# A hybrid decoder layer on one core: first gate and up passes taken by quarters in turn, state-space parameters loaded behind the statistics

## The chip, the core and the metric

The kernel runs on one core of a Trainium2 chip. The metric is the device time of one execution in microseconds (us), as the median of repeated runs. Engines are called as the profile calls them: PE (TensorE, matrix products; PEld is its loading of weights), DVE (VectorE), ACT (ScalarE), POOL (GpSimd) and SP (SyncE, which here only issues transfers). Each of them works through its own list of instructions in order.

## The reference, cut to what matters

One layer for 256 tokens of width 2048, all in float32:

```python
x = x + 0.5 * SwiGLU(RMSNorm(x))        # D_FF = 5632: gate, up, down
h = RMSNorm(x) @ W_in                   # q | k | v | u
x = x + concat(attention(q, k, v), GLU(S5(u))) @ W_out
x = x + 0.5 * SwiGLU(RMSNorm(x))

def swiglu_ffn(x, w_gate, w_up, w_down):
    return (silu(x @ w_gate) * (x @ w_up)) @ w_down
```

S5 is a state-space recurrence over 64 channel groups. Its discretised matrices depend on parameters alone (lambda, dt, B, C), so the kernel can work them out at any time before the mixer.

## The kernel before, in words

**Passes, groups, half groups.** Every weight matrix is read once. A pass (class `Pass`) is one block of 512 output columns. It multiplies all 256 tokens, as two tiles `t` of 128 rows, and gathers in two PSUM banks of 128x512, one for each tile (`acc`). It goes through the weight rows in groups of four 128-row tiles; a group is one transfer of 1 MB into a `raw` buffer, and there are three such buffers (`RAWB`). A pass over 2048 input features has four groups, called quarters here. Each group is worked in two half groups. For a half group ACT copies the raw weights, rounded, to `wh` (L286), DVE computes the rest `wl = raw - wh` (L291; L289 in halves for the first two groups), and PE does 12 products of 128x128 by 128x512: for two k tiles and two token tiles `xh*wh`, `xh*wl` and `xl*wh` (L330, L331, L332). The activations are split alike into `xth` and `xtl`. Four `wh`/`wl` pairs exist (`WB`), so ACT and DVE can be at most some three half groups ahead of PE.

**Who sets the order.** The order is written out by hand. `run` walks through the groups; `ahead` emits transfers and splits ahead of the products. After each half group `step` advances every spawned generator by one yield: everything else (normalisation, statistics, the turning of hidden values, state-space parameters) is such a generator, and a number that it yields is how many half groups it sits out.

**The start.** The input `x` is fetched as four column quarters (`res0` to `res3`, by `load_x` between the weight transfers on SP). `Normed.feed` transposes a quarter on PE (L189), and `close` scales it by the gain and splits it on ACT (L170) and DVE (L173). `warm_up` puts transposes of the identity on PE while nothing else is there. The row statistics (`squares`, L158 on ACT; `count`, ending in twelve small POOL instructions, L118 to L121) are needed only when the first gate pass is done: Silu (L363) takes 1/rms as its scale. Four accumulator banks exist (`accp`), two for each pass.

**Feed-forward 1.** It has 11 chunks `c` of 512 hidden columns, each a gate pass and an up pass. Behind an up pass DVE multiplies (L374), transposes 32x32 blocks (L134, `blocks`), and SP sends them through HBM and back (`h_d<-blocks`, L137; `sil<-h_d`, four transfers, L140); then ACT and DVE split the turned chunk (L124 and L125, `hid`). This is called the turn of chunk `c`. A turn's ACT instruction stands in ACT's list among the weight copies.

**State-space parameters** (`ssm_prepare`). POOL first issues the loads of all parameters (L433 to L449). Long chains of small DVE instructions follow, and then four pieces: in each, eight steps of three DVE products (L655 to L657), DVE transposes (L670), transfers of 1 MB from POOL (`m_d`: L667 and L673), products on PE, and on SP small transfers `k_d` (L688) and `t_d` (L691). For chunks 5 and up the turn waits until `ssm_prepare` has ended; the gate pass of chunk 7 forces its end.

The functions that the change touches and their callers:

Of the kernel before, what the change touches and what calls it, by code (L numbers as in the profile page):

```python
# [46 lines left out]
def hybrid_layer_kernel(  # L47
# [8 lines left out]
    act, vec, pe, pool, sync = nc.scalar, nc.vector, nc.tensor, nc.gpsimd, nc.sync  # L56
# [25 lines left out]
    def tps():  # L82
        return tpp.tile([P, 512], F32, name=nm("tp"), tag="tp")
# [3 lines left out]
    res = [const.tile([P, NT, 512], F32, name=f"res{n}", tag=f"res{n}") for n in range(4)]  # L87
# [135 lines left out]
    def spawn(g, delay=0):  # L223
        gens.append([g, delay])
        return g
# [22 lines left out]
    def finish(*gs):  # L248
        while any(alive(g) for g in gs):
            step()  # L250

    def run(passes, extra, start):
        groups = []
        for p in passes:
            for k0 in p.ks:
                groups.append((p, k0))
        ng = len(groups)
# [51 lines left out]
        for i, (p, k0) in enumerate(groups):  # L309
            if k0 == p.ks[0]:  # L310
                if p.pre:
                    p.pre()
                if p.opens:
                    p.box["acc"] = [tps() if p.bank == "tp" else
                                    accp.tile([P, 512], F32, name=nm("acc"), tag="acc") for _ in range(NT)]
                acc = p.box["acc"]
            for s in range(2):
                u = 2 * i + s
                ahead(u)
                h, l = wts.pop(u)  # L320
                order = [(kk, t) for kk in range(2) for t in range(NT)]
                if s == 1 and k0 == p.ks[-1]:
                    order = [(kk, t) for t in range(NT) for kk in range(2)]
                for kk, t in order:
                    k = k0 + 2 * s + kk
                    sh, sl = p.stat(k)
                    first = p.opens and k == p.ks[0]
                    last = p.done is not None and k == p.ks[-1] + 3
                    c = slice(t * P, (t + 1) * P)
                    pe.matmul(acc[t], sh[:, c], h[:, kk, :], start=first, stop=False)  # L330
                    pe.matmul(acc[t], sh[:, c], l[:, kk, :], start=False, stop=False)  # L331
                    pe.matmul(acc[t], sl[:, c], h[:, kk, :], start=False, stop=last)  # L332
                if s == 1 and k0 == p.ks[-1] and p.done:
                    spawn(call(p.done, acc), p.delay)
                step()
# [735 lines left out]
    with tc.manual_schedule():  # L1071
        xin = x[0].rearrange("(t p) d -> p t d", p=P)
        grow = slots.tile([50, P], F32, name="grow", tag="s5a")
        act.dma_start(out=grow[0:16], in_=ffn1_norm[0].rearrange("(k p) -> k p", p=P))
        sync.dma_start(out=res[0][:, :, 0:256], in_=xin[:, :, 0:256])
        vec.memset(warm, 0.0)
        act.activation(out=warm, in_=warm, func=AF.Silu)
        make_identity(nc, ident)

        def warm_up(n):  # L1080
            ps = tps()
            for _ in range(n):
                pe.transpose(ps[:, 0:P], ident, ident)

        warm_up(12)
        ps = tps()
        pe.transpose(ps[:, 0:16], grow[0:16], ident[:16, :16])
        vec.tensor_copy(out=gains["f1"], in_=ps[:, 0:16])

        def other_gains():  # L1090
            for i, g in enumerate((mix_norm, ffn2_norm)):
                pool.dma_start(out=grow[16 + 16 * i:32 + 16 * i], in_=g[0].rearrange("(k p) -> k p", p=P))
            pool.dma_start(out=grow[48:49], in_=q_norm)
            pool.dma_start(out=grow[49:50], in_=k_norm)
            pool.memset(flip, 0.0)
            pool.affine_select(out=flip, in_=flip, compare_op=ALU.not_equal, fill=1.0, base=1 - P,
                               pattern=[[1, P]], channel_multiplier=1)
            pool.memset(sgn[0:64], 1.0)
            pool.memset(sgn[64:128], -1.0)
            yield 4  # L1100
            ps = tps()
            pe.transpose(ps[:, 0:50], grow, ident[:50, :50])
            for i, key in enumerate(("mx", "f2")):
                vec.tensor_copy(out=gains[key], in_=ps[:, 16 + 16 * i:32 + 16 * i])
            knc = small([P, 1], "knc")
            vec.tensor_copy(out=knc, in_=ps[:, 49:50])
            vec.scalar_tensor_tensor(out=qkg, in0=ps[:, 48:49], scalar=1.0 / math.sqrt(HD), in1=knc,
                                     op0=ALU.mult, op1=ALU.mult)
            yield
            yield from bias_table()  # L1110

        def bias_table():
            rel = small([34, NH], "rel")
            pool.memset(rel, 1.0)  # L1114
            pool.dma_start(out=rel[0:32], in_=rel_bias)
            oh = slots.tile([34, SPAN], F32, name="oh", tag="s1a")
            pool.dma_start(out=oh, in_=bias_rows)
            yield
            yield
            ps = tps()  # L1120
            pe.matmul(ps[:NH, 0:SPAN], rel, oh, start=True, stop=True)
            bt = slots.tile([NH, SPAN], F32, name="bt", tag="s1b")
            vec.tensor_copy(out=bt, in_=ps[:NH, 0:SPAN])
            pool.dma_start(out=b_d, in_=bt)

        n1, nmix, n2 = Normed("f1"), Normed("mx"), Normed("f2")

        feeds = [n1.feed(n, True) for n in range(4)]

        def feed_input():  # L1130
            for n in range(1, 4):
                for _ in feeds[n]:
                    pass
                yield 2 if n < 3 else 1
            spawn(other_gains())
            mx["pre"] = spawn(ssm_prepare(), 1)
            for n in range(4):
                n1.squares(n)
                n1.count()
                yield  # L1140

        def start():
            next(feeds[0], None)
            if "go" not in mx:
                warm_up(4)
            if "go" in mx:
                spawn(feed_input())
            mx["go"] = True

        ff1 = ffn(n1, ffn1_w_gate[0], ffn1_w_up[0], ffn1_w_down[0], residual(nmix, 0.5), True)  # L1150
        mixp = mixer(nmix, residual(n2, 1.0))
        ff2 = ffn(n2, ffn2_w_gate[0], ffn2_w_up[0], ffn2_w_down[0], lambda n: final(n), False)

        def load_x(n):
            if n == 0:
                sync.dma_start(out=res[0][:, :, 256:512], in_=xin[:, :, 256:512])
            elif n < 4:
                sync.dma_start(out=res[n], in_=xin[:, :, n * 512:(n + 1) * 512])

        run(ff1 + mixp + ff2, load_x, start)  # L1160


# [52 lines left out]
```

## Time and profile before

| | us |
|---|---|
| median of three runs | 1836.66 |
| the runs | 1832.95, 1836.66, 1837.66 |
| the profiled execution | 1833.54 |
| its span, first to last instruction | 1831.8 |
| mean granted PE clock in it | 0.992 |

The span is shorter than the execution by 1.7 us, which lie around the program. Views of waits name the waiting instruction first, then what released it, then the total, the count and the longest. A timeline row has the start, the busy time, engine, line, operation and tiles, and in brackets the idle time ahead of it with what ended it. A row of the view of stretches has, behind its bounds and length, the busy time of each engine with its number of instructions, then the granted PE clock, the busy share of the transfer engines and GB/s.

### The profile page before, as it was taken

How to read it: one execution, taken by the hardware profiler on the slowest of the kernel's cores; microseconds unless marked ns; L12 is line 12 of the kernel's file. 1: busy time of each engine (PE TensorE's matmuls, PEld its weight loads, DVE VectorE, ACT ScalarE, POOL GpSimd, SP SyncE). 2: the span in 40 equal slices, each digit the busy share in tenths (PEclk: the TensorE clock that was granted, in tenths of full speed). 3: DMA queues.
4: the chain of work that ended last, by engine and by line, in shares of the span. 5: the costliest groups of instructions: out<-in, count | busy, mean ns of one | idle time of the engine just before them, and what ended most of it. 6: DMA issues, size and time to landing. Idle time of an engine off the chain costs nothing.

```text
span 1831.8 us, 21467 instructions
## 1 busy us (share of the span) xinstructions
PE 1798.0 (98%) x8389; PEld 1476.9 (81%) x8389; DVE 1060.3 (58%) x1382; ACT 834.7 (46%) x1071; POOL 43.4 (2%) x91
## 2 busy tenths in 40 slices
PE   8999999999999999989999999999999999999999
PEld 6788777788888888868878888888888888888887
DVE  4778788555554555534795665555555555544443
ACT  5444344444444444435667555444444444443332
POOL 2100000000000000010000001000000000000000
PEclk8999999999999999989999999999999999999999
DMA  8665788867776666599656586677767767665662
GB/s 270 208 213 191 254 264 283 262 211 213 224 218 215 209 219 216 186 255 302 186 156 250 197 246 212 195 232 217 224 212 217 219 210 225 208 222 202 202 211 103
DMA packets 220389, 401.23 MB, mean 219 GB/s; under 512 B 9580, under 2 KB 50133, under 8 KB 219136
## 3 DMA queue, kind: packets, MB, share of 16 engines
q1 hardware_dynamic: 214384, 383.29, 65.7%
q0 software_dynamic: 4080, 13.43, 2.4%
q10 hardware_dynamic: 1824, 3.15, 0.7%
q8 instruction: 65, 1.06, 0.2%
q14 instruction: 36, 0.29, 0.0%
HBM read 370.00 MB, written 32.45 MB: 220 GB/s over the span
## 4 chain that ended last, share of the span: by engine, by line
PE 84%; DVE 8%; DMA 5%; ACT 1%; issue 1%; SPq 1%; ACTq 0%; DVEq 0%
PE acc L330 27%; PE acc L331 27%; PE acc L332 27%; DVE wl L291 3%; DMA h_d<-blocks 2%; DMA sil<-h_d 1%; DMA raw<-in_ffn_w_gate_dram 1%; DVE s4b L655 1%; ACT wh L286 1%; DMA raw<-in_w_in_dram 1%; DVE s1a L768 1%; DVE s1a L769 0%; DVE slot L656 0%; DVE s4a L657 0%; DVE s4a L656 0%
## 5 line engine op out<-in xcount | busy, mean ns | idle before, releaser
L291 DVE TENSOR_TENSOR wl<-raw,wh 128x1024 fp32r<-128x1024 f32 x628 | 764.6, 1225 | 635.0 <-ACT wh L286 634.5
L286 ACT ACTIVATE wh<-raw 128x1024 fp32r<-128x1024 f32 (+1 forms) x636 | 666.2, 1057 | 820.6 <-PE acc L332 762.5
L330 PE MATMUL acc<-wh,xth 128*128 128x512 f32 x1664 | 658.7, 396 | 16.5 <-ACT wh L286 16.5
L331 PE MATMUL acc<-wl,xth 128*128 128x512 f32 x1664 | 653.9, 393 | 3.6 <-DVE wl L291 3.2
L332 PE MATMUL acc<-wh,xtl 128*128 128x512 f32 x1664 | 652.0, 392 | 0.0
L330 PEld LDWEIGHTS acc<-wh,xth 128*128 128x128 f32 x1664 | 314.9, 189 | 85.1 <-ACT wh L286 19.0
L331 PEld LDWEIGHTS acc<-wl,xth 128*128 128x128 f32 x1664 | 315.0, 189 | 74.0 <-DVE wl L291 9.7
L332 PEld LDWEIGHTS acc<-wh,xtl 128*128 128x128 f32 x1664 | 314.8, 189 | 66.1
L331 PE MATMUL acc<-wl,hid 128*128 128x512 f32 x704 | 274.0, 389 | 0.0
L330 PE MATMUL acc<-wh,hid 128*128 128x512 f32 x704 | 274.0, 389 | 0.0
L332 PE MATMUL acc<-wh,hid 128*128 128x512 f32 x704 | 273.9, 389 | 0.0
L331 PEld LDWEIGHTS acc<-wl,hid 128*128 128x128 f32 x704 | 132.1, 188 | 27.5
L332 PEld LDWEIGHTS acc<-wh,hid 128*128 128x128 f32 x704 | 132.1, 188 | 27.5
L330 PEld LDWEIGHTS acc<-wh,hid 128*128 128x128 f32 x704 | 132.1, 188 | 27.3
L125 DVE TENSOR_TENSOR hid<-sil,hid 128x512 fp32r<-128x512 f32 x44 | 28.5, 688 | 79.6 <-ACT hid L124 79.6
L124 ACT ACTIVATE hid<-sil 128x512 fp32r<-128x512 f32 x44 | 25.4, 624 | 99.4 <-DMA sil<-h_d 99.4
L374 DVE SCALAR_TENSOR_TENSOR sil<-acc,rstd,sil 128x512 f32<-128x512 f32 x44 | 30.8, 741 | 0.0
L363 ACT ACTIVATE sil<-acc,rstd 128x512 f32<-128x512 f32 x44 | 27.5, 674 | 3.8 <-POOL rel L1114 3.8
L134 DVE STREAM_TRANSPOSE blocks<-sil 128x512 f32<-128x512 f32 x44 | 28.5, 685 | 0.0
L118 POOL TENSOR_TENSOR rs_t<-rstd 128x2 f32<-128x2 f32 x9 | 5.7, 632 | 659.8 <-DVE rstd L115 659.3
L330 PE MATMUL acc<-wh,slot 128*128 128x512 f32 x48 | 18.9, 393 | 0.0
L331 PE MATMUL acc<-wl,slot 128*128 128x512 f32 x48 | 18.7, 389 | 0.0
(324 smaller groups left out, 791.0 us busy)
## 6 DMA issues: line engine op xcount, KB each, us to landing
raw<-in_ffn_w_up_dram SPq DMA_DIRECT2D x88, 1024.0 KB, 5.9
raw<-in_ffn_w_down_dram SPq DMA_DIRECT2D x88, 1024.0 KB, 5.1
raw<-in_ffn_w_gate_dram SPq DMA_DIRECT2D x87, 1024.0 KB, 5.9
raw<-in_w_in_dram SPq DMA_DIRECT2D x32, 1024.0 KB, 5.6
raw<-in_w_out_dram SPq DMA_DIRECT2D x16, 1024.0 KB, 5.6
h_d<-blocks SPq DMA_DIRECT2D x28, 512.0 KB, 7.0
sil<-h_d SPq DMA_DIRECT2D x88, 128.0 KB, 7.3
m_d<-slot POOLq DMA_DIRECT2D x4, 1024.0 KB, 7.0
```

Source lines behind the costliest of these rows:

```text
L124: act.activation(out=h, in_=src, func=AF.Copy)
L125: vec.tensor_tensor(out=l, in0=src, in1=h.bitcast(F32), op=ALU.subtract)
L134: vec.transpose(out=b[:, :, t].rearrange("p j (k c) -> p j k c", k=4), in_=src[:, t, :].rearrange("p (k j c) -> p j k c", k=4, j=4))
L286: act.activation(out=h[:, c], in_=src[:, c], func=AF.Copy)
L291: vec.tensor_tensor(out=l, in0=src, in1=h.bitcast(F32), op=ALU.subtract)
L330: pe.matmul(acc[t], sh[:, c], h[:, kk, :], start=first, stop=False)
L331: pe.matmul(acc[t], sh[:, c], l[:, kk, :], start=False, stop=False)
L332: pe.matmul(acc[t], sl[:, c], h[:, kk, :], start=False, stop=last)
L363: act.activation(out=sil[c][:, t, :], in_=acc[t], func=AF.Silu, scale=norm.scale(t))
L374: vec.scalar_tensor_tensor(out=a[:, t, :], in0=acc[t], scalar=norm.scale(t), in1=a[:, t, :], op0=ALU.mult, op1=ALU.mult)
L655: vec.tensor_tensor(out=t_, in0=zb, in1=pr, op=ALU.mult)
L768: vec.tensor_tensor(out=tm, in0=a8, in1=prev.unsqueeze(1).broadcast_to([P, 2, 2, NG]), op=ALU.mult)
```

## The change

The first eight groups are taken in another order: gate quarter 0, up quarter 0, gate 1, up 1, gate 2, gate 3, up 2, up 3. Both passes of chunk 0 are open at once, so all four accumulator banks are in use until Silu has read the gate's two. The input's quarters 1, 2 and 3 are fetched after weight groups 1, 3 and 4 of the new order. Their transposition comes at other half groups. The statistics of a quarter are taken between the quarters' feeds and no longer all behind them. `other_gains` and `ssm_prepare` are spawned after the statistics and no longer before them; so on POOL the twelve statistics instructions stand ahead of the parameter loads. The second warm-up has 14 transposes in place of 4.

```diff
     def run(passes, extra, start):
-        groups = []
-        for p in passes:
+        g, u = passes[:2]
+        groups = [(g, 0), (u, 0), (g, 4), (u, 4), (g, 8), (g, 12), (u, 8), (u, 12)]
+        for p in passes[2:]:
             for k0 in p.ks:
                 groups.append((p, k0))
...
-                acc = p.box["acc"]
+            acc = p.box["acc"]
...
             for n in range(1, 4):
                 for _ in feeds[n]:
                     pass
-                yield 2 if n < 3 else 1
+                yield
+                n1.squares(n - 1)
+                n1.count()
+                yield 3 if n == 1 else 1
+            n1.squares(3)
+            n1.count()
+            yield
             spawn(other_gains())
             mx["pre"] = spawn(ssm_prepare(), 1)
-            for n in range(4):
-                n1.squares(n)
-                n1.count()
-                yield
 
         def start():
             next(feeds[0], None)
             if "go" not in mx:
-                warm_up(4)
+                warm_up(14)
             if "go" in mx:
-                spawn(feed_input())
+                spawn(feed_input(), 2)
             mx["go"] = True
...
-            elif n < 4:
-                sync.dma_start(out=res[n], in_=xin[:, :, n * 512:(n + 1) * 512])
+            elif n in (2, 4, 5):
+                c = (n + 1) // 2
+                sync.dma_start(out=res[c], in_=xin[:, :, c * 512:(c + 1) * 512])
```

Three places show what this does to the lists; lines of the changed kernel are 1 higher from the head of `run` on, and 4 higher at the end. First SP at its start, where `res` are the input's quarters and `raw` the weight groups. Before:

```order
L1075 DMA res_83<-in_x_dram 128x2x256
L269 DMA raw_144<-in_ffn_w_gate_dram 128x512 x2
L1156 DMA res_83<-in_x_dram 128x2x256
L271 DMA raw_144<-in_ffn_w_gate_dram 128x2x512
L1158 DMA res_84<-in_x_dram 128x2x512
L273 DMA raw_150<-in_ffn_w_gate_dram 128x4x512
L1158 DMA res_85<-in_x_dram 128x2x512
L273 DMA raw_153<-in_ffn_w_gate_dram 128x4x512
L1158 DMA res_86<-in_x_dram 128x2x512
L273 DMA raw_193<-in_ffn_w_gate_dram 128x4x512
```

Now:

```order
L1076 DMA res_83<-in_x_dram 128x2x256
L270 DMA raw_144<-in_ffn_w_gate_dram 128x512 x2
L1159 DMA res_83<-in_x_dram 128x2x256
L272 DMA raw_144<-in_ffn_w_gate_dram 128x2x512
L274 DMA raw_149<-in_ffn_w_up_dram 128x4x512
L1162 DMA res_84<-in_x_dram 128x2x512
L274 DMA raw_152<-in_ffn_w_gate_dram 128x4x512
L274 DMA raw_201<-in_ffn_w_up_dram 128x4x512
L1162 DMA res_85<-in_x_dram 128x2x512
L274 DMA raw_228<-in_ffn_w_gate_dram 128x4x512
L1162 DMA res_86<-in_x_dram 128x2x512
```

A group of the up pass, which works on the input quarter that is already there, now comes between the gate's quarters, and each further input quarter is asked for later.

Second, SP at the turn of chunk 2 (`h_d`, `sil`) and the first state-space piece (`k_d`, `t_d`). Before:

```order
L137 DMA h_d_107<-blocks_1478 128x4x256
L273 DMA raw_1526<-in_ffn_w_up_dram 128x4x512
L140 DMA sil_494<-h_d_107 32x4x256 x4
L273 DMA raw_1569<-in_ffn_w_gate_dram 128x4x512
L688 DMA k_d<-slot_63_420 16x4x128 x4
L273 DMA raw_1635<-in_ffn_w_gate_dram 128x4x512
L691 DMA t_d<-k_d 256x1x128 x8
```

Now:

```order
L137 DMA h_d_107<-blocks_1470 128x4x256
L274 DMA raw_1518<-in_ffn_w_up_dram 128x4x512
L140 DMA sil_555<-h_d_107 32x4x256 x4
L274 DMA raw_1564<-in_ffn_w_gate_dram 128x4x512
L274 DMA raw_1610<-in_ffn_w_gate_dram 128x4x512
L274 DMA raw_1650<-in_ffn_w_gate_dram 128x4x512
L274 DMA raw_1687<-in_ffn_w_gate_dram 128x4x512
L689 DMA k_d<-slot_86_560 16x4x128 x4
L274 DMA raw_1749<-in_ffn_w_up_dram 128x4x512
L692 DMA t_d<-k_d 256x1x128 x8
```

The turn stands where it stood; the piece comes three weight groups, that is six half groups, later.

Third, DVE at the same turn: L134 are its block transposes, L655 to L657 the piece's products, `wl` the weight splits. Before:

```order
L291 TENSOR_TENSOR wl_1460<-raw_1358,wh_1459 128x1024
L655 TENSOR_TENSOR s4b_422<-s2a_418,slot_63_420 128x256
L656 TENSOR_TENSOR s4a_421<-s2a_418,slot_63_420 128x16x16
L657 TENSOR_TENSOR s4a_421<-s4a_421,s4b_422 128x16x16
L134 STREAM_TRANSPOSE blocks_1478<-sil_494 128x4x128 x2
L291 TENSOR_TENSOR wl_1482<-raw_1358,wh_1481 128x1024
```

Now:

```order
L637 TENSOR_TENSOR dmask<-dmask,ident 128x16
L638 TENSOR_TENSOR dmask<-dmask,ident 128x16
L292 TENSOR_TENSOR wl_1450<-raw_1344,wh_1449 128x1024
L656 TENSOR_TENSOR s4b_562<-s2a_558,slot_86_560 128x512
L657 TENSOR_TENSOR s4a_561<-s2a_558,slot_86_560 128x16x32
L658 TENSOR_TENSOR s4a_561<-s4a_561,s4b_562 128x16x32
L134 STREAM_TRANSPOSE blocks_1470<-sil_555 128x4x128 x2
L292 TENSOR_TENSOR wl_1474<-raw_1344,wh_1473 128x1024
```

The transposes stood behind the seventh of the piece's eight steps; they stand behind the first. From the turn of chunk 6 on the lists of both kernels agree.

## The prediction

> **What bounds the kernel now.** I read the head of the page first, then the timeline at the places where the view of waits has PE waiting.
>
> ```profile
> span 1831.8 us, 21467 instructions
> PE 1798.0 (98%) x8389; PEld 1476.9 (81%) x8389; DVE 1060.3 (58%) x1382; ACT 834.7 (46%) x1071; POOL 43.4 (2%) x91
> ```
>
> PE sets the time: it is busy for 98% and idle for 34 us. The change neither adds nor removes a product, so it can only remove or add waits and slow clock. Behind the turn of chunk 6 both lists agree; only what lies ahead of it, some 370 us, can change. The start in the timeline:
>
> ```profile
> 5.24 0.92 PE L1083 MATMUL tp<-ident 128*128 128x128 f32 x4
> 8.35 0.63 PE L189 MATMUL tp<-ident,res 128*128 128x128 f32 x4 [2.18 <-DMA res<-in_x_dram]
> 20.82 2.19 ACT L286 ACTIVATE wh<-raw 128x512 fp32r<-128x512 f32 x4 [5.46 <-DMA raw<-in_ffn_w_gate_dram]
> 21.50 0.79 PE L330 MATMUL acc<-wh,xth 128*128 128x512 f32 x1 [4.54 <-ACT wh L286]
> 30.38 0.39 PE L330 MATMUL acc<-wh,xth 128*128 128x512 f32 x1
> 33.10 1.03 PE L189 MATMUL tp<-ident,res 128*128 128x128 f32 x8
> ...
> 5.00:10.00 5.00, 2.82 (x15) 2.40 (x14) 2.19 (x5) 2.86 (x7) 3.96 (x7) 0.93 0.86 283
> 10.00:15.00 5.00, 5.00 (x22) 4.01 (x22) 2.30 (x5) 2.11 (x6) 3.04 (x5) 0.73 1.06 251
> 20.00:25.00 5.00, 3.50 (x8) 2.48 (x9) 2.50 (x4) 2.19 (x4) 0.00 (x0) 0.50 1.04 385
> 25.00:30.00 5.00, 5.00 (x25) 4.16 (x24) 2.94 (x4) 3.46 (x6) 0.00 (x0) 0.86 1.05 387
> ```
>
> A half group takes 33.10 - 30.38 = 2.72 us at full clock, a feed's eight transposes 1.0. PE stands 4.54 us for the gate's second quarter of weights. Behind each pause the granted clock falls: 0.93 and 0.73 after the pause at 6.2 to 8.3, 0.50 and 0.86 after the second. The first costs 0.07 x 5 + 0.27 x 5 = 1.7 us. The second costs 0.5 x 3.5 (PE works from 21.5) + 0.14 x 5 = 2.4.
>
> Why are the weights late?
>
> ```profile
> DMA packets 1681, 2.35 MB, mean 235 GB/s; under 512 B 236, under 2 KB 811, under 8 KB 1681
> ...
> q0 software_dynamic: 784, 1.82, 23.1%
> raw<-in_ffn_w_gate_dram SPq DMA_DIRECT2D x3, 1024.0 KB, 18.0
> ```
>
> By 10 us 2.35 MB had come; in the first 30 us POOL's queue q0 moved 1.82 MB, mostly of parameters, while a weight group took 18.0 us to land. From 20 us on, without it, 385 GB/s came.
>
> Farther on, PE waits for ACT, and ACT for the turn of a chunk (first two rows: PE between 100 and 500 us):
>
> ```profile
> PE acc L330 <- ACT wh L286: 5.4, 4, 2.8
> PE acc L331 <- DVE wl L291: 2.7, 4, 0.8
> ...
> 97.57 1.15 ACT L124 ACTIVATE hid<-sil 128x512 fp32r<-128x512 f32 x2 [3.60 <-DMA sil<-h_d]
> 193.88 1.15 ACT L124 ACTIVATE hid<-sil 128x512 fp32r<-128x512 f32 x2 [9.95 <-DMA sil<-h_d]
> 243.10 1.15 ACT L124 ACTIVATE hid<-sil 128x512 fp32r<-128x512 f32 x2 [6.51 <-DMA sil<-h_d]
> 291.56 1.15 ACT L124 ACTIVATE hid<-sil 128x512 fp32r<-128x512 f32 x2 [5.71 <-DMA sil<-h_d]
> 346.58 1.15 ACT L124 ACTIVATE hid<-sil 128x512 fp32r<-128x512 f32 x2 [5.73 <-DMA sil<-h_d]
> ...
> 197.18 0.80 PE L330 MATMUL acc<-wh,xth 128*128 128x512 f32 x1 [2.81 <-ACT wh L286]
> 198.44 0.79 PE L331 MATMUL acc<-wl,xth 128*128 128x512 f32 x1 [0.46 <-DVE wl L291]
> 348.73 0.50 PE L330 MATMUL acc<-wh,xth 128*128 128x512 f32 x1 [1.32 <-ACT wh L286]
> 349.99 0.51 PE L331 MATMUL acc<-wl,xth 128*128 128x512 f32 x1 [0.76 <-DVE wl L291]
> ```
>
> The rows of ACT are the turns of chunks 0, 2, 3, 4 and 5. A wait of 3.6 us does not reach PE; one of 5.7 or more does, since the weight copies stand behind it in ACT's list. The long four are those with a state-space piece beside them. For chunk 2:
>
> ```profile
> 175.57 0.51 SPq L137 DMA_DIRECT2D h_d<-blocks  x1
> 177.62 1.17 POOL L667 DMA_DIRECT2D m_d<-slot  x1 [113.09 <-issue]
> 182.03 0.79 POOL L673 DMA_DIRECT2D m_d<-s4b  x1 [3.24 <-DVE s4b L670]
> 182.85 2.32 SPq L140 DMA_DIRECT2D sil<-h_d  x4
> ...
> 327.49 5.72 SPq L691 DMA_DIRECT2D t_d<-k_d  x8
> ...
> 195.00:200.00 5.00, 2.36 (x5) 1.56 (x6) 3.68 (x5) 5.00 (x9) 0.00 (x0) 0.70 0.16 29
> 200.00:205.00 5.00, 5.00 (x16) 3.92 (x15) 4.93 (x8) 1.63 (x2) 0.00 (x0) 0.61 1.02 339
> 350.00:355.00 5.00, 5.00 (x15) 3.96 (x16) 3.34 (x3) 2.11 (x3) 0.00 (x0) 0.66 0.78 253
> ```
>
> Two transfers of 1 MB from POOL go out between the turn's way out and its way back. Chunk 2 costs 2.81 + 0.46 = 3.3 us idle and, at clocks of 0.70 and 0.61, 0.30 x 5 + 0.39 x 5 = 3.4, less some 0.2 that was idle anyway: 3.2. Chunk 5 costs 2.1 idle and 0.34 x 5 = 1.7. Of the 8.1 us idle 2.7 are left for chunks 3 and 4.
>
> **The change, part by part.**
>
> *Order of the quarters, loads off POOL.* With up quarter 0 second, PE needs x quarter 0 (0.5 MB) and two weight groups (2.1 MB) for its first four half groups, until 8.7 (the row at 8.35 and its transposes) + 4 x 2.7 + 1.0 = 20.5 us. At 387 GB/s behind the 2.35 MB at 10 us, up quarter 0 has landed at 10.7 us, x quarter 1 at 12.1, gate quarter 1 at 14.8. The half groups of the two weight groups start at 14.2 and 20.5; splitting takes ACT and DVE about 2 us ahead of a first product. No stall is left: -4.5 and its clock, -2.4. The queue keeps ahead: 1.6 MB (a group and an input quarter) take 4.1 us, and PE works longer on them. The tightest place is x quarter 1, whose DVE splits I put at 20.5 with PE there at 20.5 to 20.8; a miss would be under a microsecond. I take 0.4 off.
>
> *Warm-up of 14.* Ten more transposes take 2.3 us at the pace of the row at 5.24 (0.92 for 4), 1.3 at that of 33.10 (1.03 for 8). They lie in the pause of 2.2 us ahead of 8.35, so they cost from nothing to 0.1. If the pause shrinks so far that the clock stays, 1.7 is saved; if not, nothing. I take 1.7 less 0.7 for a pause that is only half filled: -1.0 to -1.7, say -1.4.
> The Trainium skill (TensorE: Matmul & The Clock Gate, Part 4) says that transposes do not count as busy PE, so the gate would not open for them. By it this term is nil. The trace disagrees as far as it goes: four transposes took 0.92 at 5.24 and 0.63 at 8.35, with only transposes before them.
>
> *Statistics.* The same eight ACT instructions, earlier. PE needs them at Silu, whose two banks are wanted by half group 16, at about 8.7 + 16 x 2.7 + 4 = 56 us; three half groups lie between the last statistics and that. If that cover were gone, each us would be a us of PE. Cost 0.
>
> *Parameter loads behind the statistics on POOL.*
>
> ```profile
> 6.39 0.54 POOL L441 DMA_DIRECT2D s2b<-in_ssm_b_im_dram  x1
> 45.69 0.19 POOL L118 TENSOR_TENSOR rs_t<-rstd 128x2 f32<-128x2 f32 x1 [30.55 <-DVE rstd L115]
> ...
> s2b<-in_ssm_b_im_dram POOLq DMA_DIRECT2D x1, 256.0 KB, 9.6
> ```
>
> POOL's statistics started at 45.7. Now the last square stands behind half group 9 on PE, 39 us, with some 4 us on ACT and DVE behind it: 43, done at about 47. PE's list has a transpose of `s2b` behind half group 18, at 64 us. Before, that load went out 6.4 us into the span, all of POOL's own start included, and took 9.6 us on crowded queues: 47 + 6.4 + 9.6 = 63. The cover is 1 us or more; I take 0, at most 2 lost. DVE's chains stand as much later as PE's lists do.
>
> *Pieces six half groups later.* The turn of chunk 2 loses its neighbour: its `m_d` now go out behind `sil` has landed. That of chunk 3 too: its piece comes behind it, the one before is a turn's length ahead. For chunk 4 the first `m_d` leaves together with `sil`; I leave half. For chunk 5 nothing changes, since its turn waits for the last piece in both kernels. So -3.3 - 3.2 - 1.4 - 0.7 = -8.6.
>
> DVE has a part in it too:
>
> ```profile
> 252.52 1.22 DVE L291 TENSOR_TENSOR wl<-raw,wh 128x1024 fp32r<-128x1024 f32 x1
> 253.80 0.50 PE L331 MATMUL acc<-wl,xth 128*128 128x512 f32 x1
> 255.59 1.22 DVE L291 TENSOR_TENSOR wl<-raw,wh 128x1024 fp32r<-128x1024 f32 x1
> ```
>
> In a piece DVE needs 255.59 - 252.52 = 3.07 us for a half group, 0.35 more than PE. Its lead pays for that; after the stalls of chunks 3 and 4 the lead is gone and PE goes at DVE's pace (five and three half groups in the timeline, 8 x 0.35 = 2.8 us). I take back half: -1.4. Against it, the turns of chunks 2, 3 and 4 now put their 1.3 us of transposes into pieces, and the pieces' predecessors meet the turns of chunks 0 and 1: +1.6 for leads used up (0 to +5). The middle gives -8.4, between -12 (only chunk 5 left) and 0.
>
> **Sum.** Start -4.5 - 2.4 + 0.4 - 1.4 = -7.9, rounded to -8.0; between -4 and -9. Middle -8.4. Together -16.4: 1833.5 becomes 1817.1. The median stands 3.1 above the profiled execution, the lowest run 0.6 below it; I add half of 3.1 and predict **1818.5 us**.
>
> **Rivals.**
> 1. *The pieces find other turns.* Every chunk passes somewhere, the transfers are as many, and chunk 4's collision or `t_d` ahead of chunk 3 takes over. For it: chunk 5, with `t_d` out at 327 to 333 and its wait at 341 to 347, costs 3.8 us without an `m_d`. Against it: the turn of chunk 0, without a piece, costs nothing. Middle 0: 1833.5 - 8 + 1.5 = 1827.
> 2. *The first weights stay late.* If queue SP is held up for its buffers, half the stall and its clock remain: start -4, 1822.5.
> 3. *The warm-up does not hold the clock*: the transposes fill the pause and the half clock at 9 to 13 us stays all the same, +1.4: 1820. For it: the clock fell there though 16 transposes had gone before. Against it: it had risen before that. (The rule of the Trainium skill named above, TensorE: Matmul & The Clock Gate, Part 4, would have it so.)
> 4. *Everything goes*, chunk 5 excepted: -9 and -12: 1814.
> 5. *Slower: DVE without a lead.* Each of 32 piece steps at 0.35 over PE's pace gives 11.2 us, the STT, transposes and splits of four turns (1.4 + 1.3 + 1.3) 16: 27 us on PE, where the same stretch now loses 8.1 + 4.9 + 2.8 = 16. With the four ACT waits unchanged (8.1) that is +19 - 8 = +11: 1846. It decides if the lead at the head of a piece is nil; against it, PE waits for `wl` only four times between 100 and 500 us, 2.7 us in all, each behind a wait for ACT; the first piece, whose lead was whole, has none.
>
> **How the numbers follow.** Forecast 0.50, rivals 0.18, 0.08, 0.08, 0.11 and 0.05. The range 1810 to 1829 holds the forecast with its bounds and rivals 1 to 4, and leaves out 5 and the tails. A measurement of this kernel tells 0.3% (5.5 us) from no change: below 1831 is faster. Only rival 5, a part of rival 1 and misses in the start lead elsewhere: faster 0.88, same 0.07, slower 0.05.
>
> **What would show it.** No row of PE waiting over 1 us between 9 and 60 us, and the weight groups landing in under 10 us. ACT's L124 waits below 4 us for chunks 2 and 3, about 5 for chunk 4, 5.7 for chunk 5, and a full clock between 190 and 340 us. It is wrong if PE waits for `s2b` at 60 us, if L331 waits on `wl` over many half groups in a piece, or if an L124 wait of over 6 us stands beside an `m_d`.

## The result and the profile after

| | before | changed |
|---|---|---|
| median of the runs that were compared, us | 1836.78 | 1821.85 |
| the runs of the changed kernel | | 1816.77, 1820.39, 1823.30, 1824.86 |
| ratio of the medians, 95% interval | | 0.992 (0.9892 to 0.9947) |
| the profiled execution | 1833.54 | 1824.86 |

The change makes the kernel faster by 0.8%, 14.9 us; 1818.5 was forecast, between 1810 and 1829. The profiled execution is the slowest of the four, and that of the kernel before lay 3.2 below the median in the table: the two profiles differ by 8.7 us only, which matters for the accounts below. The head of the page:

```profile
span 1823.1 us, 21486 instructions
PE 1793.5 (98%) x8399; PEld 1477.4 (81%) x8399; DVE 1059.9 (58%) x1382; ACT 834.3 (46%) x1071; POOL 44.1 (2%) x91
```

**The start.** The timeline of the changed kernel, PE's second warm-up and its transposes of the input's second piece, the first weight copies of up quarter 0 and gate quarter 1, POOL's first statistics and the `s2b` load; then the view of stretches; then that of transfers, of the first 30 us:

```profile
5.25 2.14 PE L1084 MATMUL tp<-ident 128*128 128x128 f32 x14
8.03 0.63 PE L189 MATMUL tp<-ident,res 128*128 128x128 f32 x4 [0.65 <-DMA res<-in_x_dram]
12.00 2.19 ACT L287 ACTIVATE wh<-raw 128x512 fp32r<-128x512 f32 x4 [1.43 <-DMA raw<-in_ffn_w_up_dram]
16.15 2.01 ACT L287 ACTIVATE wh<-raw 128x1024 fp32r<-128x1024 f32 x2 [1.95 <-DMA raw<-in_ffn_w_gate_dram]
42.57 0.19 POOL L118 TENSOR_TENSOR rs_t<-rstd 128x2 f32<-128x2 f32 x1 [41.25 <-DVE rstd L115]
52.45 0.54 POOL L442 DMA_DIRECT2D s2b<-in_ssm_b_im_dram  x1
```

```profile
5.00:10.00 5.00, 4.35 (x28) 3.88 (x27) 2.50 (x6) 3.18 (x8) 0.00 (x0) 1.00 0.93 317
10.00:15.00 5.00, 5.00 (x24) 4.12 (x23) 3.98 (x8) 2.76 (x6) 0.00 (x0) 1.00 1.05 389
...
280.00:285.00 5.00, 0.44 (x1) 0.29 (x1) 1.76 (x3) 3.74 (x6) 0.00 (x0) 0.76 0.37 148
285.00:290.00 5.00, 4.54 (x12) 3.33 (x12) 5.00 (x9) 3.44 (x6) 0.00 (x0) 0.56 0.61 193
```

```profile
raw<-in_ffn_w_up_dram SPq DMA_DIRECT2D x4, 1024.0 KB, 6.8
raw<-in_ffn_w_gate_dram SPq DMA_DIRECT2D x3, 1024.0 KB, 8.8
```

PE's pause ahead of the input is 0.65 us in place of 2.18, the clock stays at 1.00, the copying of gate quarter 1 begins at 16.15, some four microseconds ahead of PE's need, and the 4.54 us wait is gone. A group lands in 6.8 to 8.8 us by the medians of the view, not 18.0.

**The middle.** ACT's turns of chunks 0 to 5 in the timeline of the same profile, what PE then waits for, and what SP and POOL issue around chunk 4; behind them, of the view of transfers, the two rows of that place:

```profile
91.45 1.15 ACT L124 ACTIVATE hid<-sil 128x512 fp32r<-128x512 f32 x2 [7.13 <-DMA sil<-h_d]
135.74 1.15 ACT L124 ACTIVATE hid<-sil 128x512 fp32r<-128x512 f32 x2 [5.29 <-DMA sil<-h_d]
179.52 1.16 ACT L124 ACTIVATE hid<-sil 128x512 fp32r<-128x512 f32 x2 [3.22 <-DMA sil<-h_d]
229.24 1.16 ACT L124 ACTIVATE hid<-sil 128x512 fp32r<-128x512 f32 x2 [5.87 <-DMA sil<-h_d]
281.26 1.15 ACT L124 ACTIVATE hid<-sil 128x512 fp32r<-128x512 f32 x2 [12.87 <-DMA m_d<-s4b]
352.07 1.16 ACT L124 ACTIVATE hid<-sil 128x512 fp32r<-128x512 f32 x2 [5.65 <-DMA sil<-h_d]
...
284.56 0.80 PE L331 MATMUL acc<-wh,xth 128*128 128x512 f32 x1 [5.39 <-ACT wh L287]
285.82 0.80 PE L332 MATMUL acc<-wl,xth 128*128 128x512 f32 x1 [0.46 <-DVE wl L292]
356.54 0.50 PE L332 MATMUL acc<-wl,xth 128*128 128x512 f32 x1 [1.82 <-DVE wl L292]
...
261.58 0.50 SPq L137 DMA_DIRECT2D h_d<-blocks  x1
268.58 4.09 SPq L140 DMA_DIRECT2D sil<-h_d  x4
268.69 1.12 POOL L668 DMA_DIRECT2D m_d<-slot  x1 [32.65 <-DVE slot L658]
273.36 0.77 POOL L674 DMA_DIRECT2D m_d<-s4b  x1 [3.55 <-DVE s4b L671]
```

```profile
m_d<-s4b POOLq DMA_DIRECT2D x1, 1024.0 KB, 8.8
sil<-h_d SPq DMA_DIRECT2D x4, 128.0 KB, 9.6
```

Chunk 2 has lost its stall (9.95 became 3.22). Chunk 4 has one: 12.87 us on ACT, 5.85 on PE, and behind it a half clock (0.56 in the row from 285 on; the records show half from 282.6 to 289.5). The row names `m_d<-s4b` as the releaser, but that transfer left at 273.36 and took 8.8 us, so it landed at 282.2, behind the end of the wait; the last of the four `sil` left at 271.5 and took 9.7, which is 281.2. ACT waited for `sil`; `m_d` shares a semaphore that the instruction also names. What `m_d` does, as I read it, is make `sil` slow: its first transfer leaves 0.1 us behind the first of them. The table of distances farther down holds this against seven more profiles.

**Where the time went, by stretch.** I took the moment at which PE begins a half group's products with `wl`, in both profiles, and subtracted. A second profile of the unaltered changed kernel (the first experiment) stands beside it. Half groups are counted from the program's start.

| stretch (half groups) | forecast, us | first profile | second profile |
|---|---|---|---|
| start (to 28) | -8.0 | -9.8 | -10.1 |
| turns of chunks 0, 1 (28 to 56) | up to +1.6 for leads | +2.7 | +2.3 |
| chunk 2 (56 to 72) | -6.5 | -7.9 | -7.9 |
| chunk 3 and DVE's pace behind it (72 to 90) | -2.8 | -1.4 | -3.7 |
| chunk 4 (90 to 104) | -0.7 | **+5.4** | **+5.0** |
| chunk 5 (104 to 120) | 0 | +1.1 | -1.9 |
| all behind it | 0 | +1.1 | +0.2 |
| sum | -16.4 | -8.7 | -16.1 |

### The profile page after: what moved, and what is told of

Read it like the earlier page. It is cut to its first block, busy times and chain, and to the rows that moved or that the text cites. A ratio compares the mean times of both kernels' runs of the same rounds, so it can differ in the third digit from the quotient of the medians.

```text
span 1823.1 us, 21486 instructions
## 1 busy us (share of the span) xinstructions
PE 1793.5 (98%) x8399; PEld 1477.4 (81%) x8399; DVE 1059.9 (58%) x1382; ACT 834.3 (46%) x1071; POOL 44.1 (2%) x91
## 4 chain that ended last, share of the span: by engine, by line
PE 80%; issue 11%; DVE 4%; DMA 3%; ACT 1%; POOL 0%; SPq 0%; ACTq 0%; POOLq 0%
PE acc L332 26%; PE acc L331 26%; PE acc L333 26%; DVE wl L292 1%; DMA raw<-in_w_in_dram 1%; DMA u_d<-s4a 1%; DVE s1a L769 1%; DMA h_d<-blocks 0%; DMA m_d<-s4b 0%; ACT wh L287 0%; DVE s1a L770 0%; DMA res<-in_x_dram 0%; DVE slot L771 0%; DMA slot<-m_d 0%; PE tp L189 0%
## 5 line engine op out<-in xcount | busy, mean ns | idle before, releaser
L331 PE MATMUL acc<-wh,xth 128*128 128x512 f32 x1664 | 657.0, 395 | 13.1 <-ACT wh L287 12.9
L124 ACT ACTIVATE hid<-sil 128x512 fp32r<-128x512 f32 x44 | 25.4, 624 | 104.5 <-DMA sil<-h_d 91.6
L134 DVE STREAM_TRANSPOSE blocks<-sil 128x512 f32<-128x512 f32 x44 | 28.6, 687 | 0.0
```

The costliest lines, as they stand in the source:

```text
L124: act.activation(out=h, in_=src, func=AF.Copy)
L134: vec.transpose(out=b[:, :, t].rearrange("p j (k c) -> p j k c", k=4), in_=src[:, t, :].rearrange("p (k j c) -> p j k c", k=4, j=4))
```

## The experiments

All times are medians; each ratio is to the kernel before on the same chip, with its 95% interval. The kernel before had 1835.80 beside the first four, 1834.62 beside the next four, 1834.45 beside the ninth and tenth, 1835.78 beside the last two. Kernels of different groups ran on different chips, so a difference of medians between groups is good to some 1.5 us only; where it matters I also give the difference of the gains, each over the kernel before on its own chip.

| kernel | median, us | range | ratio |
|---|---|---|---|
| changed kernel, again | 1818.39 | 1816.08 to 1819.55 | 0.9904 (0.9888 to 0.9919) |
| old order, late loads | 1828.20 | 1822.15 to 1831.95 | 0.9955 (0.9937 to 0.9972) |
| new order, early loads | 1829.52 | 1826.60 to 1831.62 | 0.9967 (0.9955 to 0.9979) |
| changed, pieces 3 later | 1818.47 | 1817.17 to 1820.25 | 0.9909 (0.9894 to 0.9924) |
| changed, split 3 later | 1810.73 | 1808.78 to 1811.46 | 0.9869 (0.9856 to 0.9882) |
| changed, split and pieces 3 later | 1809.09 | 1808.81 to 1810.78 | 0.9864 (0.9850 to 0.9877) |
| old order, late loads, same pieces | 1820.31 | 1817.35 to 1823.48 | 0.9923 (0.9911 to 0.9936) |
| changed, warm-up of 4 | 1819.31 | 1816.67 to 1822.67 | 0.9913 (0.9897 to 0.9928) |
| old order, late loads, split | 1815.71 | 1812.97 to 1818.40 | 0.9900 (0.9887 to 0.9914) |
| before, split alone | 1817.68 | 1816.95 to 1820.56 | 0.9914 (0.9901 to 0.9928) |
| old order, all else | 1811.98 | 1810.83 to 1814.97 | 0.9878 (0.9863 to 0.9893) |
| old order, all else, warm-up of 4 | 1813.24 | 1812.80 to 1814.34 | 0.9883 (0.9866 to 0.9899) |

**1. The changed kernel again.** No edit.

> The changed kernel once more, unaltered, with a new profile and more runs. My theory: the stall behind the turn of chunk 4 belongs to the order of the transfers (two 1 MB m_d leave within 5 us of sil), so it is there in every execution: an ACT wait of 10 to 13 us at L124 near 281 us, PE idle 6 us, and a half clock for 6.8 us behind it; time 1818 to 1823. Rival: that stall was an accident of one execution; then the new profile has no L124 wait over 6 us ahead of chunk 5, and its span is some 8 us shorter.

The timeline of its profile, ACT's turn of chunk 4 and PE behind it:

```profile
277.17 1.15 ACT L124 ACTIVATE hid<-sil 128x512 fp32r<-128x512 f32 x2 [12.13 <-DMA m_d<-s4b]
280.47 0.79 PE L331 MATMUL acc<-wh,xth 128*128 128x512 f32 x1 [4.42 <-ACT wh L287]
```

The stall is no accident: it is there again, 4.9 us on PE where I expected 6, and a half clock of 6.8 us from 279.7 on. The span is 7.5 us shorter all the same, mostly because chunks 3 and 5 cost less. So the middle is worth between 0 and -6 from one execution to the next, and a single pair of profiles measures it badly.

**2. Which part mends the start: late loads alone.**

```diff
-            spawn(other_gains())
-            mx["pre"] = spawn(ssm_prepare(), 1)
             for n in range(4):
                 n1.squares(n)
                 n1.count()
                 yield
+            spawn(other_gains())
+            mx["pre"] = spawn(ssm_prepare(), 1)
```

> The kernel before, with only one part of the change: other_gains and ssm_prepare are spawned behind the statistics. The order of the quarters and the warm-up are the old ones. My theory (the parameter loads held the weights up): weight groups land in under 10 us, the wait of 4.54 us at 21.5 shrinks below 1.5, and the start gains 5 to 7 us. Rival (the order of the quarters is what matters): over 3 us of the stall stay and the start gains under 3. The pieces come four half groups later here, so their m_d leave with the turn of chunk 3 as they do with that of chunk 4 in the changed kernel: if the distance from m_d to sil makes the wait, the L124 wait of chunk 3 is 10 to 13 us, that of chunk 2 about 6 and that of chunk 4 about 10, and the middle gains nothing: 1829 to 1832 in all. If the distance does not matter, the waits stay as before (9.95, 6.51, 5.71).

The view of transfers of its first 30 us, and in its timeline the turns of chunks 2, 3 and 4:

```profile
raw<-in_ffn_w_gate_dram SPq DMA_DIRECT2D x3, 1024.0 KB, 10.0
```

```profile
183.18 1.15 ACT L124 ACTIVATE hid<-sil 128x512 fp32r<-128x512 f32 x2 [5.85 <-DMA sil<-h_d]
231.99 1.15 ACT L124 ACTIVATE hid<-sil 128x512 fp32r<-128x512 f32 x2 [9.91 <-DMA sil<-h_d]
282.06 1.15 ACT L124 ACTIVATE hid<-sil 128x512 fp32r<-128x512 f32 x2 [9.51 <-DMA sil<-h_d]
```

PE has no wait over 0.4 us between 9 and 60 us; by half group 28 it is 9.1 us ahead of the kernel before, more than the 5 to 7 expected, with the old order and a warm-up of 4. That profile is a favourable one: it is the fastest run of the six, 6 us below their median, its input's second piece came at 7.24 us, the earliest of all profiles, and the clock stayed full. Three later kernels have the same start (experiments 7, 9 and 12), and they are only 5.7, 6.0 and 5.9 us ahead there, each with a stretch of half clock. So the late loads alone give 6 to 9 us of a start gain of 8 to 10 (-9.8, -10.1, and -9.2, -8.8, -8.1 in experiments 4 to 6). The turns came out as the distance from `m_d` to `sil` said: 5.85, 9.91 and 9.51 where about 6, 10 to 13 and about 10 were expected; the median of 1828.20 is 0.8 below the 1829 expected at the least.

**3. The other half: new order, early loads.** `ssm_prepare` runs as far as its loads at the start, the rest where it was.

```diff
         def feed_input():
+            mx["loads"] = ssm_prepare()
+            next(mx["loads"])
...
-            mx["pre"] = spawn(ssm_prepare(), 1)
+            mx["pre"] = spawn(mx["loads"], 4)
```

> The changed kernel, with the loads of the state-space parameters issued on POOL at the start again; all that follows them stays where it is. My theory: about 1.8 MB beside the first weights, so with 250 GB/s until 20 us gate quarter 1 lands near 25 us where PE needs it at 20.5; a stall of 3 to 6 us and its half clock come back, 5 to 8 us over the changed kernel: 1826 to 1829. Rival (the new order covers a late group by itself): under 2 us lost. The waits of the turns stay as in the changed kernel.

PE in its timeline, a stretch, and POOL's queue of its first 30 us:

```profile
20.61 0.80 PE L331 MATMUL acc<-wh,xth 128*128 128x512 f32 x1 [4.66 <-ACT wh L287]
```

```profile
10.00:15.00 5.00, 4.32 (x18) 3.02 (x17) 2.17 (x4) 1.24 (x3) 0.01 (x1) 1.00 1.04 250
```

```profile
q0 software_dynamic: 656, 1.81, 22.3%
raw<-in_ffn_w_up_dram SPq DMA_DIRECT2D x2, 1024.0 KB, 14.7
```

The stall is back, 4.66 us, and the half clock with it: by half group 28 this kernel stands where the kernel before stands (-0.1). 1829.52 against 1818.39, half a microsecond more than the most that I expected: the place of 1.8 MB of parameter loads is worth 11 us, and the order of the quarters does not cover for it.

**4. Pieces three half groups later.**

```diff
-            mx["pre"] = spawn(ssm_prepare(), 1)
+            mx["pre"] = spawn(ssm_prepare(), 4)
```

> The changed kernel with ssm_prepare spawned three half groups later, so that every m_d of chunks 2 to 4 leaves behind sil has landed (for chunk 4, three half groups or 8 us behind its issue). My theory (m_d beside sil makes the wait): L124 waits of chunks 2, 3 and 4 below 5 us, no PE wait at 285 and no half clock there; against the changed kernel 5.9 of idle and 3.4 of clock less 0.2, so -8 where the stall is: 1812 to 1815. Rival (some piece always meets some turn): another L124 wait over 6 us ahead of chunk 5, and the time stays within 2 us of the changed kernel. Chunk 5 keeps its wait of 5.7 in both.

SP in its timeline ahead of the turn of chunk 3, and that turn:

```profile
211.37 5.42 SPq L692 DMA_DIRECT2D t_d<-k_d  x8
216.84 0.60 SPq L137 DMA_DIRECT2D h_d<-blocks  x1
221.12 1.74 SPq L140 DMA_DIRECT2D sil<-h_d  x4
...
228.03 1.15 ACT L124 ACTIVATE hid<-sil 128x512 fp32r<-128x512 f32 x2 [8.51 <-DMA sil<-h_d]
```

The rival won: 1818.47, no gain. Chunk 4's wait fell from 12.1 to 7.46, but now the eight `t_d` of the piece before hold SP's list for 5.42 us, `h_d` of chunk 3 leaves only behind them, and its turn waits 8.51 us without any `m_d` near. With pieces every 14 half groups and turns every 16, something of a piece met some turn in every place that I tried. My theory was too narrow: the `m_d` are not the only neighbour that makes a turn late, here the `t_d` ahead of it on SP do so too. Nor is chunk 4's 7.46 explained by the `m_d`: here their first left 8.0 us behind the first `sil`, at 276.6, and the last `sil` landed 1.1 us after that.

**5. The split three half groups later.** In ACT's and DVE's lists of the first feed-forward alone.

```diff
-    def by_blocks(src, dst):
+    def by_blocks(src, dst, rest=3):
...
-        yield 3
+        yield rest
...
-                    turned = yield from by_blocks(a, a.rearrange("p t x -> p (t x)"))
+                    turned = yield from by_blocks(a, a.rearrange("p t x -> p (t x)"), 6 if first else 3)
```

> The changed kernel, with the split of a turned chunk (L124 on ACT, L125 on DVE) put three half groups, 8.2 us, later into the lists of the first feed-forward; the transfers stay where they are. My theory (the transfers are late, but only ACT's order makes a stall of it): the L124 waits of 6.7, 4.8, 3.1, 5.3, 12.1 and 5.9 us of the changed kernel's second profile shrink by 8.2 to nothing but some 4 for chunk 4, no PE wait over 1 us between 60 and 360 us and no half clock in that stretch; against 1818.4 that is 4.4 + 0.5 + 0.8 + 0.9 of idle and 3.4 of clock, about -10: 1807 to 1811. Rival (DVE or SP takes over as the next limit): PE waits for wl instead, and under 3 us are gained: 1815 to 1819.

PE's waits between 60 and 420 us in the view of waits (the only row), and ACT's turn of chunk 4:

```profile
PE acc L332 <- DVE wl L292: 1.0, 1, 1.0
```

```profile
276.41 1.15 ACT L124 ACTIVATE hid<-sil 128x512 fp32r<-128x512 f32 x2 [2.30 <-DMA sil<-h_d]
```

The `sil` of chunk 4 are as late as ever, landing at 276.3, 11.7 us behind the first one's issue; but ACT comes to the split later, waits 2.30 us for them in place of 12.13, and PE does not feel it. No half clock is left between 6 and 791 us. 7.7 us are gained on experiment 1 by the medians (6.5 by the gains), and both kernels are beaten. The Trainium skill says it as a rule (DMA: Bandwidth & Descriptors, Rules for kernel authors): issue a transfer early and wait for it late. Here the wait, a place in a list, was 8 us too early.

**6. Both.** The edits of 4 and 5 together.

> The same with the pieces also three half groups later, as in the run of that name. My theory: once ACT does not stand in line behind the turn, the place of the m_d and t_d transfers is worth nothing, and this kernel comes within 2 us of the one with the split alone. Rival (the transfers also hold up the weights themselves): the two differ by more than 3 us.

1809.09, 1.6 us from the split alone, with ranges that overlap: once ACT does not stand behind the turn, it is worth nothing that can be measured which of these two places the pieces' transfers have. It has the lowest median of all.

**7. Old order, late loads, pieces where the changed kernel has them.** The edit of 2, with a delay of 3 in place of 1.

> The kernel before, with the parameter loads behind the statistics and the pieces at the very half groups of the changed kernel; the order of the quarters, the input's transfers and the warm-up of 4 are the old ones. The profiles so far give the late loads the whole start gain (-9.3 by half group 24 with the old order; -0.1 with the new order and early loads). My theory now: the order of the quarters and the longer warm-up are worth nothing by themselves beyond the place that they give to the pieces, so this kernel is as fast as the changed one: 1817 to 1821, with an L124 wait of 12 us at chunk 4. Rival: the order has a share of its own in the middle; then it stays near the 1828 of the run with the old order and late loads.

The turn of chunk 4 in its timeline:

```profile
278.94 1.15 ACT L124 ACTIVATE hid<-sil 128x512 fp32r<-128x512 f32 x2 [10.74 <-DMA sil<-h_d]
```

1820.31: two half groups in the place of the pieces are worth 7.9 us by the medians (1828.20 before; 6.7 by the gains), and with them the old order comes to 1.9 us of the changed kernel (3.1 by the gains), with ranges that overlap.

**8. The warm-up undone.** `warm_up(14)` becomes `warm_up(4)`.

> The changed kernel with the second warm-up at 4 transposes as before. My theory as predicted: the clock falls to half behind the pause ahead of 8 us again, 1.4 us lost. What the run with the old order and late loads suggests: there four transposes and a pause of 1.68 us kept the clock full from 4.64 us on, since the input came 1.1 us earlier without the parameter loads beside it; then nothing is lost and the warm-up is worth nothing here.

The same stretches of its profile as above:

```profile
5.00:10.00 5.00, 2.30 (x13) 2.00 (x12) 2.08 (x4) 2.37 (x6) 0.00 (x0) 0.83 0.91 320
10.00:15.00 5.00, 5.00 (x20) 4.01 (x20) 4.03 (x8) 3.57 (x7) 0.00 (x0) 0.83 1.02 383
```

The half clock is back for one stretch of 3.4 us, 0.17 x 5 twice, 1.7 us, behind a pause of 2.70. The medians (1819.31 and 1818.39) do not tell so little apart. The forecast of -1.4 stands. The case against it, the second kernel above, kept its clock since its input came at 7.24 us and the pause was 1.68; but that is not the work of the late loads, as I had it. With them and a warm-up of 4 the same piece came at 7.98, 8.03, 8.04 (experiments 7, 9, 12) and 8.38 us (here), without them at 7.88 (experiment 10) and 8.35 (before): its time scatters.

**9. Two edits to the kernel before: late loads and the split.**

> The kernel before with two edits and nothing else: the parameter loads behind the statistics (as in the run with the old order and late loads) and the split of the turned chunk three half groups later. The quarters' order and the warm-up are the old ones, the m_d leave where they made waits of 9.9 and 9.5 us. My theory (these two causes hold all that there is to gain here): start -7.5 to -9.5, depending on whether the half clock near 9 us comes, and all idle and slow clock of the turns, 8.2 + 4.9 = 13: 1834.6 less 21 to 23, so 1811 to 1814. Rival (the new order of the quarters is needed for the split to pay): 1816 or more.

PE between 60 and 420 us in the view of waits:

```profile
PE acc L331 <- DVE wl L291: 3.2, 4, 1.3
```

1815.71, 1.7 above what I expected. At the start its profile is only 6.0 us ahead by half group 28, not 7.5 to 9.5: its clock was at half until 13.55, for its products take 0.63 us each up to 12.75 and some 0.4 from 13.6 on. And in the last two pieces, between 257 and 308 us, PE waits for DVE four times. No wait for ACT is left. Here rival 5 of the prediction, DVE without lead, shows in a small size.

**10. The split alone in the kernel before.**

> The kernel before with the later split alone; the parameter loads stay at the start. My theory (the two causes are apart and add up): the stall of 4.5 us at 21.5 and its half clock stay, the L124 wait of chunk 2 shrinks from 9.95 to some 2 and the others to nothing, so 8.2 of idle and 4.9 of clock go: 1834.6 less 13, 1820 to 1823. Rival (the pieces take the lead of DVE, so PE waits for wl as soon as it does not wait for ACT): under 8 us gained, 1827 or more.

The start in its timeline, and PE between 60 and 420 us in the view of waits (the only row):

```profile
21.28 0.79 PE L330 MATMUL acc<-wh,xth 128*128 128x512 f32 x1 [4.95 <-ACT wh L286]
```

```profile
PE acc L331 <- DVE wl L291: 1.2, 2, 0.8
```

One number makes the kernel before as fast as the whole change does: 1817.68. It gained 16.8, more than the 13 expected. In the profile 14.6 us of it lie between half groups 28 and 120: 6.9 of waits (8.1 became 1.2), the 4.9 of clock that the prediction had worked out, and 2.8 more, as much as the prediction had put down to DVE's pace; that DVE's lead, once no stall uses it up, pays for this is my reading. The start is untouched, stall and all. Nor do the two causes simply add up: the late loads are worth 7.6 us without the split and 2.0 with it (1817.68 to 1815.71). By the profiles the start still gains 5.1 by half group 28, and 5.0 are lost again up to 120, where the pieces come four half groups later and PE waits 3.2 us for DVE in place of 1.2.

**11 and 12. The old order with everything else, and with the old warm-up.** The edits of 7 and 5 on the kernel before, with `warm_up(14)` and with `warm_up(4)`.

> The kernel with the split 3 later (1810.73) except for one thing: the quarters and the input's transfers stand in the old order. The loads are late, the pieces at the changed kernel's half groups, the warm-up has 14. My theory: the order of the quarters is worth nothing by itself, so 1809 to 1813. Rival: it has a share, and this kernel stays at the 1815.7 of the old order with loads and split.

> The same with the warm-up at 4. My theory: what the kernel with the old order, loads and split lacked against 1811 was in part the place of its pieces (in its profile PE waits for wl four times, 3.2 us, between 257 and 308 us) and in part the clock at the start; with the pieces moved 2 to 4 us come back, and the warm-up of 4 costs 1.7 against 14 where the half clock behind the pause near 8 us comes: 1811 to 1814. Rival: neither matters, and it stays at 1815.7.

The stretch from 10 to 15 us of the first and of the second:

```profile
10.00:15.00 5.00, 5.00 (x28) 4.08 (x26) 3.89 (x10) 3.69 (x10) 0.00 (x0) 1.00 1.05 396
```

```profile
10.00:15.00 5.00, 5.00 (x23) 4.12 (x22) 2.40 (x6) 2.55 (x7) 0.00 (x0) 0.78 1.05 393
```

Both came out in the range expected. 1811.98 against 1810.73 with the new order: by the medians the order of the quarters is worth 1.2 us by itself, by the gains 0.1, and the ranges overlap. The warm-up is worth 1.3 by the medians and 1.7 by the clock. With the pieces moved, 2.5 us of what the ninth kernel lacked came back (3.8 by the gains), within the 2 to 4 expected.

## Why the prediction came out as it did

**The total** of 1818.5 lies between the two medians of the changed kernel, 1821.85 and 1818.39. Its parts were not all as good.

**Start, -8.0: the mechanism was right, the size small, the credit misplaced.** The stall, its half clock and the pause of 2.18 us all shrank as told; -9.8 and -10.1 were measured, beyond the bound of -9; in part the input's second piece came sooner, at 8.03 and 7.46 us in place of 8.35, which scatters from run to run. But the step "Order of the quarters, loads off POOL" worked both out as one. The loads alone give 5.7 to 9.1 (experiments 2, 7, 9, 12), with the longer warm-up and the old order 7.8 (experiment 11), with everything 8.1 to 10.1; the order with the longer warm-up but without the late loads gives 0.1 (experiment 3). Its own evidence, a weight group that took 18.0 us while q0 moved 1.82 MB, pointed to the loads; what the order adds to them does not stand out from the scatter. Rival 2 is out.

**Warm-up, -1.4**: 1.7 by the clock, 1.3 by the medians. Rival 3 is out: in all six profiles with the warm-up of 14 and the late loads the clock is full from its first record (4.84 to 7.45 us) until past 230 us, and up to that record PE had done nothing but transposes. For these float32 transposes that also goes against the rule of the Trainium skill that the prediction set beside it (TensorE: Matmul & The Clock Gate, Part 4).

**Statistics and parameter loads, 0 and 0**: right. POOL's statistics began at 42.57, as estimated, `s2b` left at 52.45, and no wait of PE names it. What was overlooked is another load behind the statistics, `oh` of the bias table: PE waits for it 0.2 us in the second profile, up to 2.1 in experiment 7.

**Chunk 2, -6.5**: right, -7.9. **Chunk 3 with DVE's pace, -2.8**: -1.4 and -3.7; its L124 wait of 5.87 and 5.28 is over the 4 that I named.

**Chunk 4, -0.7: this is the step that failed.** "For chunk 4 the first m_d leaves together with sil; I leave half." It took the wait to be the smaller the later the `m_d` leave. It is largest when they leave with `sil` or shortly ahead. The table has all turns of chunks 2 to 4 with an `m_d` near, from eight profiles (before, changed twice, experiments 2, 3, 4, 7, 8); the distance is from the first `sil` to the first `m_d`, the landing from the issue of the first `sil` to the landing of the last.

| distance, us | turns | L124 wait, us | landing, us |
|---|---|---|---|
| -18.7, -14.1 | 2 | 5.7, 6.5 | 5.4, 5.2 |
| -5.6, -5.2 | 2 | 9.5, 10.0 | 10.5, 10.9 |
| -0.1 to +0.2 | 6 | 9.9 to 12.9 | 10.3 to 12.6 |
| +3.0 to +4.2 | 3 | 5.9 to 6.4 | 5.5 to 6.2 |
| +5.5 to +6.4 | 3 | 5.3 to 6.5 | 6.6 to 7.0 |
| +8.0 (experiment 4) | 1 | 7.5 | 9.1 |
| +13.7, +13.8 | 5 | 3.1 to 3.2 | 6.2 to 6.4 |

(Experiment 4's chunk 3, at +15.9 and 8.5 us, is the one behind `t_d`.) The landing shows what the `m_d` do: it takes over 10 us only where they leave with `sil` or 5 to 6 us ahead. The waits of 5.3 to 6.5 us go with landings of 5.2 to 7.0, the last row's 3.1 to 3.2 with 6.2 to 6.4, so a slow landing does not explain that difference; it stays open. Nor does a landing need an `m_d` to be long: for chunk 0, with none under way, it took 5.2 to 9.8 us in the same profiles. So the term was +5 in place of -0.7, and the criterion that I had given for being wrong, an L124 wait of over 6 us beside an `m_d`, was met. Rival 1 had named this very collision, and the `t_d` of experiment 4 too; its middle of 0 is what the first profile shows, -6 the second.

**Why the total held nevertheless.** The miss of 6.1 and 5.7 us at chunk 4 in the two profiles was met by the start (-2), chunk 2 (-1.4) and, in the second profile, chunks 3 and 5 (-2.8 together). That is luck of opposite signs, not accuracy.

**Rival 5, DVE without lead**, did not happen here: PE waited for `wl` for 3.8 and 2.1 us in the two profiles between 60 and 420 us. Experiment 9 shows that it is not far off.

**What the prediction did not see at all** is that a late transfer need not cost anything. It treated "the weight copies stand behind it in ACT's list" as given, and asked only which transfers would be late. Moving that one place is worth as much as the whole change.

**Left open.** The wait of chunk 0's turn rose from 3.60 to 7.13 and 6.69, some 1.0 to 1.5 us on PE; it was 3.0 to 3.5 in experiments 4 and 7, 6.4 to 6.5 in 2, 3 and 8, and no edit explains that. So are the 1.6 us between experiments 5 and 6, if they are real, and the waits of 5.3 to 6.5 us in the table.

## What to carry to other kernels

An instruction that waits for a round trip through memory should stand in its engine's list behind everything that others need before the round trip can be sure to have ended; here three half groups were worth as much as the whole change. Before pricing the transfers that make such a wait long, ask whether the wait has to stand there. And where a change moves two things at once, price each alone: late loads gave the start most of what it gained, the longer warm-up 1 to 2 us, and the order nothing that stood out from the scatter. Do it with more than one profile: four profiles of the same start here differ by 3.4 us.

## What the runs showed of the hardware

**POOL's parameter loads slowed SP's weight groups down.** Without POOL's 1.8 MB a 1 MB weight group landed in 6.7 to 10.9 us (changed kernel, experiments 2 and 11); the groups beside them took 14.7 (experiment 3) to 18.0 (before); between 10 and 15 us 389 GB/s came, with them 250. That agrees with the Trainium skill (DMA: Bandwidth & Descriptors, Issuing engines are not separate DMA queues), by which transfers of all issuing engines run on the same 16 and interleave. That the mixture brings so much less in all I had not expected.

**Short pauses are enough for the half clock, and where they fall decides.** Pauses at the start of 1.96 (experiment 7), 2.14 (12), 2.18 (before), 2.49 (10) and 2.70 (8) each brought 3.4 us of half clock; pauses of 0.65 (changed), 1.53 (5), 1.64 (6) and 1.68 (2) did not. (Behind the 1.72 of experiment 9 the clock was at half as well, but its records begin with the rise at 13.55, so they do not tell whether it fell there or had not yet risen.) At 356.5 us in the changed kernel a wait of 1.82 was followed by one too, and so were two waits of 0.98 and 0.76 within 2 us in experiment 4. But the length alone does not decide. These two waits, the first of experiment 7 and the second of experiment 2, are longer, and the clock stays full behind both:

```profile
64.52 0.80 PE L1121 MATMUL tp<-oh,rel 34*8 34x384 f32 x2 [2.10 <-DMA oh<-in_bias_rows_dram]
285.36 0.50 PE L330 MATMUL acc<-wh,xth 128*128 128x512 f32 x1 [2.38 <-ACT wh L286]
```

In every trace the recorded changes of the clock lie whole multiples of 3.413 us apart. I cut all fourteen traces into windows along these moments and added up PE's idle time in each window at full clock: all 33 with 1.96 us or more were followed by half clock, none with 1.72 or less was, and of 20 in between 10 were. The wait of 2.10 fell into two windows, as 1.19 and 0.91; that of 2.38 lay across two with 1.55 and 1.58 us of idle time. The Trainium skill gives about 3 us as the longest gap to leave (TensorE: Matmul & The Clock Gate, Why this matters for your kernels); in these runs the shortest single wait with a half clock behind it was 1.74 us (experiment 11, at 920 us), and 1.96 within one window was always too long.
